# More channel pairs by the usual products while the input's forms are made, in the ffn of a fp32 decoder trunk

## The chip, the core and the metric

The kernel runs on one core of one Trainium2 chip. The metric is the device time of one execution in microseconds (us), lower is better: 1331.78 us is the median of three runs of the kernel before (1330.34 to 1333.43).

## What is computed

A decoder trunk of two layers, on 512 rows of a prompt and 8 x 8 rows of samples (576 columns T in the kernel, which keeps the activations transposed, channels on partitions). Each layer is a mixer and a gated ConvFFN; the change is in the ConvFFN, which is the larger part of both layers:

```python
D_MODEL = 1024
D_FF = 3 * D_MODEL
FFN_CONV = 3

def _conv_ffn(xn, prev, w_up, cw, cb, w_down):
    u = jnp.einsum("btd,df->btf", xn, w_up)
    uc, new_prev = _causal_dwconv(u, prev, cw, cb)
    g, val = jnp.split(uc, 2, axis=-1)
    return jnp.einsum("btf,fd->btd", jax.nn.gelu(g) * val, w_down), new_prev
```

Here xn is the RMS-normed input, w_up is 1024 x 6144, w_down 3072 x 1024. Layer 0 has an attention and RG-LRU mixer (mixer_ab), layer 1 a pooling mixer (mixer_pool). All is float32.

## The kernel before

run() calls mixer_ab, pool_setup (GpSimd makes the band matrices of the pooling mixer), ffn(0), mixer_pool, ffn(1). A fp32 product is made as three products of a high and a low part (hi x hi, hi x lo, lo x hi), each of 128 x 128 weights with 288 columns, two halves for the 576. A weight block is loaded to `wraw`, then split: ScalarE copies the high part, VectorE subtracts it for the low one (split, or wform in the units; both write `whl`).

**ffn, up projection.** The 6144 channels are 24 pairs of blocks of 128: index i, s = 0 the gate, s = 1 the value. For each pair, u is the product, conv (L1256) makes a causal convolution of width 3 of it (ScalarE, then two VectorE operations, L1268 and L1269, on tile t), gate (L1272) applies GELU, multiplies, and leaves the product as a pair hh, hl in `hs[i]`.

- The pairs i = 0 and 1 go by up_pair (L1283): the usual products of mm3, 8 blocks of the input x 3 x 2 halves = 48 matmuls for each s, from the input's parts xs that are there already; the norm's factor rb is multiplied in when u is read out of `pu`.
- The other 22 pairs go by 22 units. A unit n covers the blocks i and i + 1 of one s and forms a 2 x 2 product by seven products instead of eight (named 1 to 7, in the order 1, 2, 5, 6, 7, 4, 3; 12 matmuls each, in the banks X, Y, Z). For that it needs sums and differences of the weights' four quarters (a11 to a22, made on GpSimd, L1390 to L1399) and of the input's quarters.
- The input's forms are made by normed() (L1320), called after up_pair(0), and sums() (L1337), called after up_pair(1). For four chunks c, normed makes xn[c] and xn[c + 4] (VectorE, L1323, 128 x 576), copies their high parts to xa and xb (ScalarE, L1325) and the low parts (VectorE, L1326), then makes four mixed sums in place (GpSimd, L1329 to L1332, 128 x 288). sums() splits what is then in xn to xh and xl.

**ffn, down projection.** The 3072 rows are six blocks q of 512, by eight blocks m of output channels: dn_w loads (`wd`) and splits, dn_p (L1488) makes 4 k x 3 x 2 = 24 matmuls (L1495) and add_x adds the result into xT (VectorE, L711).

**What sets the order.** A list `plan` (L1521 to L1551) holds the products of the units and the down blocks in the order of TensorE. Weights are prepared three entries ahead. Blocks q < 5, 40 in all, stand in it: one after product 6 of each unit from n = 3, one after its product 5 from n = 2, and the rest behind the last unit. After it comes the last block, q = 5 (L1573 on), three m at a time, k = 0, 1 of all three first. tick() runs one step of a background list (`bg`): loads and transposes of convolution states (states), and the transposes and stores of the convolution's tails (tails). A scheduler then fixes the order of each engine's queue from the program and its priorities.

**Space.** xn shares its buffers with hh and hl (tags "hh", "hl", 6 each). xa and xb lie in ffn's own pool.

Of the kernel before, what the change touches and what calls it, by code (L numbers as in the profile page):

```python
# [43 lines left out]
class Trunk:  # L44
# [1179 lines left out]
    def ffn(self, l, after, first=0):  # L1224
# [7 lines left out]
        b8 = lambda t: t.rearrange("p (b j) -> p b j", j=8)  # L1232
        with self.tc.tile_pool(name="ff", bufs=2, reuse_waits="tile") as fp:
            stT = fp.tile([P, 48, 16], F32, name="fstT", bufs=1)
# [8 lines left out]
            for a in (1, 7, 2, 8, 3, 9, 4, 10, 5, 11):  # L1243
                self.bg.append(lambda a=a: states(a))
            if l == 0:
                for a in range(2):
                    self.bg.append(lambda a=a: self.pool_states(fp, a))
# [24 lines left out]
            def gate(i, tg, tv):  # L1272
                A.activation(tg[:, 0:592], tg[:, 0:592], AF.Gelu_apprx_tanh)
                hf_ = self.sm.tile([P, T], F32, name="hf", tag="sq", bufs=2)
                V.tensor_tensor(hf_[:, 0:NP], tg[:, 0:NP], tv[:, 0:NP], MUL)  # L1275
                V.tensor_tensor(b8(hf_[:, NP:T]), b10(tg, 0, 8), b10(tv, 0, 8), MUL)
                hh = fp.tile([P, T], F32R, name="hh", tag="hh", bufs=6)
                hl = fp.tile([P, T], F32R, name="hl", tag="hl", bufs=6)
                A.copy(hh, hf_)
                V.tensor_tensor(hl, hf_, hh.bitcast(F32), SUB)  # L1280
                hs[i] = (hh, hl)

            def up_pair(i):  # L1283

                if i % 2 == 0:
                    for s in range(2):
                        if self.up0:
# [26 lines left out]
            xa, xb = [], []  # L1314
            for p in range(2):
                xa.append(fp.tile([P, 4, HT], F32R, name="xa", tag=f"xa{p}", bufs=1))
                xb.append(fp.tile([P, 4, T], F32R, name="xb", tag=f"xb{p}", bufs=1))
            X = {}

            def normed():  # L1320
                for c in range(4):
                    for k in (c, c + 4):
                        V.scalar_tensor_tensor(xn[k], self.xT[:, k, :], self.g_ffn(l, k), self.rb, MUL, MUL)  # L1323
                    for x, v in ((xa, xn[c][:, 0:HT]), (xb, xn[c + 4])):
# [45 lines left out]
            def load(n, f, h):  # L1370

                if n > 21:
# [3 lines left out]
                c0 = n % 2 * DFF + (2 + n // 2 * 2 + f) * P  # L1376
                nc.sync.dma_start(quarter(n, f, h), up[:, 4 * h:4 * h + 4, c0:c0 + P])
# [5 lines left out]
            def unit(n):  # L1383

                s, i = n % 2, 2 + n // 2 * 2
                a11, a12, a21, a22 = [quarter(n, f, h) for f in range(2) for h in range(2)]
# [77 lines left out]
                def p3(w):  # L1464
# [36 lines left out]
            def tails(q, s):  # L1501
# [17 lines left out]
            sums()  # L1519

            units = {}  # L1521
            downs = deque((q, m) for q in range(5) for m in range(8))
            plan = []
# [10 lines left out]
            put(0, "5")  # L1534
            for n in range(22):
                nx = n + 1 if n < 21 else None
# [28 lines left out]
            for j, (kind, a, b) in enumerate(plan):  # L1565
# [3 lines left out]
                else:  # L1569
                    dn_p(a, b, ready.pop(j))  # L1570
                if kind == "down" or a < 3:
                    self.tick()

            after(None)
            ms = [range(0, 3), range(3, 6), range(6, 8)]
            ws = {}
            for m in range(3):
                ws[m] = dn_w(5, m)
            self.psum(8)
            for g in ms:  # L1580
                ps = {}
                for m in g:
                    ps[m] = dn_p(5, m, ws[m], None, range(2))
                for m in g:
                    dn_p(5, m, ws[m], ps[m], range(2, 4))
                    if m + 3 < 8:
                        ws[m + 3] = dn_w(5, m + 3)
                    after(m)
                    if len(self.bg) > 1:
                        self.tick()  # L1590
                    if self.mid:
                        self.mid.popleft()()
            self.flush()
# [27 lines left out]
    def run(self):  # L1621
        self.load_x()
        self.mixer_ab()
        with self.tc.tile_pool(name="pb", bufs=1, reuse_waits="tile") as pb:
            self.pool_setup(pb)
            self.ffn(0, self.then_norm(lambda m: self.g_mix(1, m)), first=4)
            self.xg_end()
            self.mixer_pool(pb)
        self.xg_end()
# [212 lines left out]
```

## Time and profile before

| | us |
|---|---|
| median of three runs | 1331.78 |
| lowest and highest | 1330.34, 1333.43 |
| the profiled execution | 1323.17 |
| its span in the trace | 1321.5 |

The profiled execution is 8.6 us under the median of the runs. In the trace an ffn can be cut into four windows: the products of the first two pairs (305.6 to 337.4 us in ffn(0), 823.7 to 856.1 in ffn(1)), the first units until their pace is steady (to 422.6, to 943.7), the rest of the units with the down blocks (to 752.2, to 1273.2), the last block (to 788.0, to 1314.9). Between the two ffn is mixer_pool, ahead of them mixer_ab.

How to read a row: PE is TensorE's matmuls, PEld its weight loads, DVE VectorE, ACT ScalarE, POOL GpSimd, SP the engine that issues most loads. "A <- B" behind an idle time says that the engine waited for B. PEclk is the clock that TensorE was granted, 1.00 being 2.4 GHz. Busy matmuls are pipelined, so their durations overlap; the pace is better read from counts over a window.

### The profile page before, as it was taken

To read this page: it belongs to the slowest core of one execution; us is meant where nothing else is said; L and a number is where in the kernel's file an instruction comes from. 1 tells how busy PE (TensorE), PEld (TensorE's weight loads), DVE (VectorE), ACT (ScalarE), POOL (GpSimd) and SP (SyncE) were. 2 spreads that over 40 slices of the span, in tenths; PEclk is the share of its full clock that TensorE was granted. 3 is DMA by queue.
4 is the path that set the end of the run, shared out by engine and by line. 5 is a ranking of instruction groups with operands and counts; after the bars stand their busy time and mean duration, and the time that the engine had idled before them with its cause. 6 is when DMAs were issued, how large, how long until landed. Compare 5 with 4: busy or idle time off the path is not lost.

```text
span 1321.5 us, 23545 instructions
## 1 busy us (share of the span) xinstructions
PE 1242.3 (94%) x8894; PEld 1175.5 (89%) x8894; DVE 1050.5 (79%) x1939; ACT 691.3 (52%) x1365; POOL 500.9 (38%) x738
## 2 busy tenths in 40 slices
PE   7999989999788999999999999967999999999988
PEld 6988878898578999999999989857999999999987
DVE  5857879887977888888888868886798888888862
ACT  5657467764444554555455446344455555455532
POOL 2240064381843444444443002474343444344300
PEclk9999999999688999999999999968999999999999
DMA  5323343332122333223322202302233233323122
GB/s 156 101 67 100 98 148 89 90 107 85 43 58 66 95 92 93 85 89 90 97 89 75 82 17 70 117 22 73 60 94 98 81 94 93 94 77 98 58 65 74
DMA packets 153478, 111.69 MB, mean 85 GB/s; under 512 B 9217, under 2 KB 144521, under 8 KB 153356
## 3 DMA queue, kind: packets, MB, share of 16 engines
q1 hardware_dynamic: 149220, 101.69, 25.6%
q0 software_dynamic: 3072, 8.46, 2.3%
q8 instruction: 70, 1.15, 0.4%
q14 instruction: 44, 0.36, 0.1%
q10 hardware_dynamic: 1072, 0.04, 0.0%
HBM read 104.14 MB, written 6.25 MB: 84 GB/s over the span
## 4 chain that ended last, share of the span: by engine, by line
PE 70%; DVE 16%; ACT 4%; POOL 3%; issue 3%; DMA 2%; SPq 0%; ACTq 0%; DVEq 0%; POOLq 0%
PE mmb L1495 19%; PE pX L1365 18%; PE pY L1365 9%; PE mmb L143 6%; PE mmb L588 5%; PE pZ L1365 4%; DVE whl L1359 4%; DVE t L1268 2%; PE pu L143 2%; DVE hl L1280 1%; PE mmb L911 1%; DVE t L1269 1%; ACT whl L1358 1%; DVE hf L1275 1%; DMA wraw<-in_ffn_w_up 1%
## 5 line engine op out<-in xcount | busy, mean ns | idle before, releaser
L1495 PE MATMUL mmb<-hh,whl 128*128 128x288 f32 x1536 | 285.8, 298 | 13.2 <-DVE xT L711 7.5
L1495 PEld LDWEIGHTS mmb<-hh,whl 128*128 128x128 f32 x1536 | 232.6, 190 | 14.6 <-DVE xT L711 8.0
L1365 PE MATMUL pX<-xh,whl 128*128 128x288 f32 x1056 | 240.3, 303 | 3.7 <-ACT c L1450 2.7
L1359 DVE TENSOR_TENSOR whl<-wraw,whl 128x512 fp32r<-128x512 f32 x264 | 210.8, 819 | 20.4 <-ACT whl L1358 17.5
L1358 ACT CAST whl<-wraw 128x512 fp32r<-128x512 f32 x264 | 156.9, 619 | 93.3 <-PE mmb L1495 51.6
L1365 PEld LDWEIGHTS pX<-xh,whl 128*128 128x128 f32 x1056 | 182.1, 194 | 5.6 <-ACT c L1450 3.6
L1495 PE MATMUL mmb<-hl,whl 128*128 128x288 f32 x768 | 166.5, 298 | 6.5 <-DVE hl L1280 6.5
L1365 PE MATMUL pX<-xl,whl 128*128 128x288 f32 x528 | 159.4, 302 | 5.3 <-DVE xl L1343 5.3
L711 DVE TENSOR_TENSOR xT<-mmb,xT 128x288 f32<-128x288 f32 x208 | 87.0, 449 | 69.9 <-PE mmb L1495 68.1
L1263 POOL COPY ut<-u 128x18 f32<-128x18 f32 x96 | 36.5, 380 | 259.2 <-DVE u L1427 257.5
L1495 PEld LDWEIGHTS mmb<-hl,whl 128*128 128x128 f32 x768 | 124.2, 190 | 8.6 <-DVE hl L1280 8.4
L1268 DVE SCALAR_TENSOR_TENSOR t<-u,par,t 128x592 f32<-128x592 f32 x96 | 99.9, 1042 | 24.6 <-ACT t L1267 24.2
L1365 PE MATMUL pX<-xa,whl 128*128 128x288 f32 x528 | 90.4, 318 | 18.9 <-ACT xa L1325 10.2
L1365 PEld LDWEIGHTS pX<-xl,whl 128*128 128x128 f32 x528 | 102.2, 194 | 6.5 <-DVE xl L1343 6.5
L1267 ACT ACTIVATE t<-u,par 128x592 f32<-128x592 f32 x96 | 84.4, 882 | 36.9 <-DVE u L1427 34.0
L1365 PEld LDWEIGHTS pX<-xa,whl 128*128 128x128 f32 x528 | 80.4, 205 | 22.6 <-ACT xa L1325 11.9
L1269 DVE SCALAR_TENSOR_TENSOR t<-u,par,t 128x592 f32<-128x592 f32 x96 | 96.0, 1000 | 1.5
L1390 POOL TENSOR_TENSOR wraw<-wraw 128x512 f32<-128x512 f32 x44 | 65.3, 1484 | 74.4 <-DMA wraw<-in_ffn_w_up 74.4
L1365 PE MATMUL pZ<-xb,whl 128*128 128x288 f32 x528 | 86.4, 309 | 1.6 <-ACT whl L1358 1.3
L1399 POOL TENSOR_TENSOR wraw<-wraw,d 128x512 f32<-128x512 f32 x44 | 67.8, 1542 | 42.7 <-DVE whl L1359 42.6
L1365 PEld LDWEIGHTS pZ<-xb,whl 128*128 128x128 f32 x528 | 77.1, 197 | 3.9 <-ACT whl L1358 1.7
L1365 PE MATMUL pY<-xb,whl 128*128 128x288 f32 x528 | 78.7, 298 | 0.0
(440 smaller groups left out, 2821.8 us busy)
## 6 DMA issues: line engine op xcount, KB each, us to landing
wraw<-in_ffn_w_up SPq DMA_DIRECT2D x176, 256.0 KB
wd<-in_ffn_w_down SPq DMA_DIRECT2D x48, 512.0 KB
wraw<-in_ab_w_in SPq DMA_DIRECT2D x9, 1024.0 KB
wraw<-in_ab_w_out SPq DMA_DIRECT2D x4, 1024.0 KB
wraw<-in_ffn_w_up SPq DMA_DIRECT2D x4, 1024.0 KB
xt<-in_x_prompt SPq DMA_DIRECT2D x4, 512.0 KB
out_y_p<-y SPq DMA_DIRECT2D x8, 256.0 KB
wraw<-in_ab_w_in SPq DMA_DIRECT2D x2, 512.0 KB
```

Source lines behind the costliest of these rows:

```text
L143: nc.tensor.matmul(ps[hf][:, 0:HT], w[:, k, :], x[:, hf * HT:(hf + 1) * HT], start=(n == 0 and j == 0), stop=(n == K - 1 and j == 2))
L588: PE.matmul(ps[i], x[:, i * P:(i + 1) * P], w[:, k2, :], start=(k == 0 and j == 0), stop=(k == 7 and j == 2))
L711: self.nc.vector.tensor_tensor(x, ps[hf][:, 0:HT], x, ADD)
L1267: A.activation(t, u[:, 2:594], AF.Identity, scale=self.fw(l, 2, ch), bias=self.fb(l, ch))
L1268: V.scalar_tensor_tensor(t, u[:, 1:593], self.fw(l, 1, ch), t, MUL, ADD)
L1269: V.scalar_tensor_tensor(t, u[:, 0:592], self.fw(l, 0, ch), t, MUL, ADD)
L1358: A.copy(f[:, 0], v)
L1359: V.tensor_tensor(f[:, 1], v, f[:, 0].bitcast(F32), SUB)
L1365: PE.matmul(ps[:, 0:HT], w[:, a, k, :], x[b][:, k, :], start=(start and k == 0 and j == 0), stop=(k == 3 and j == 2), skip_group_check=True)
L1390: G.tensor_tensor(a21, a11, a21, SUB)
L1399: G.tensor_tensor(a12, a12, st["d"], SUB)
L1495: PE.matmul(ps[hf][:, 0:HT], w[:, a, k, :], hs[4 * q + k][b][:, hf * HT:(hf + 1) * HT], start=(k == 0 and j == 0), stop=(k == 3 and j == 2))
```

## The change

Six pairs instead of two go by up_pair. The twelve steps of normed (norm, parts, mixed, for each of four chunks) become entries of a list `todo`; two of them are taken after each s of the pairs 1 to 3, and the mixed sums are on VectorE instead of GpSimd. sums() runs inside pair 5. In the pairs 4 and 5, one down block of q = 0 is made after each s (down_now). 18 units are left, with 28 down blocks in the plan: two for the units 1 to 10, 12 and 14, one for 0, 11, 13 and 15, none for 16 and 17. The last 1024 rows (hs 16 to 23) form one last block: eight k for each m, its weights loaded 1 MB for two m; m = 0 and 1 first make k = 0 to 5 of both, then k = 6 and 7, the others go by mm3. hh and hl get nine buffers; xa and xb lie in a side pool that is closed after the units. pool_setup and pool_states move from ahead of ffn(0) to its end. Two empty background steps stand before the transposes of each tail.

```diff
-            xn = [fp.tile([P, T], F32, name="xn", tag=("hh", "hl")[c // 4], bufs=6) for c in range(8)]
+            xn = [fp.tile([P, T], F32, name="xn", tag=("hh", "hl")[c // 4], bufs=9) for c in range(8)]
...
+                    if i:
+                        for _ in range(2):
+                            if todo:
+                                todo.popleft()()
+                    if i >= 4:
+                        down_now()
+                if i == 5:
+                    while todo:
+                        todo.popleft()()
+                    sums()
...
+                def mixed(c):
                     a0, a1 = xn[c][:, 0:HT], xn[c][:, HT:T]
                     b0, b1 = xn[c + 4][:, 0:HT], xn[c + 4][:, HT:T]
-                    G.tensor_tensor(a0, a1, a0, SUB)
-                    G.tensor_tensor(a1, b1, a1, SUB)
-                    G.tensor_tensor(b1, b1, a0, SUB)
-                    G.tensor_tensor(b0, b0, b1, SUB)
...
+                    V.tensor_tensor(a0, a1, a0, SUB)
+                    V.tensor_tensor(a1, b1, a1, SUB)
+                    V.tensor_tensor(b1, b1, a0, SUB)
+                    V.tensor_tensor(b0, b0, b1, SUB)
+
+                for c in range(4):
+                    for f in (norm, parts, mixed):
+                        todo.append(lambda f=f, c=c: f(c))
...
+                                self.bg.extend([lambda: None] * 2)
...
+            def down_now():
+                q, m = downs.popleft()
+                dn_p(q, m, dn_w(q, m))
+                self.tick()
+
             self.psum(3)
-            for i in range(2):
+            fq = side.enter_context(self.tc.tile_pool(name="fq", bufs=1, reuse_waits="tile"))
+            for i in range(6):
                 up_pair(i)
                 if i == 0:
-                    normed()
-            self.up0 = None
+                    normed(fq)
+                if i == 3:
+                    for s in range(2):
+                        self.bg.append(lambda s=s: tails(0, s))
...
-                if n >= 3:
+                if 1 <= n <= 10 or n in (12, 14):
                     put_down()
...
-                if n >= 2:
+                if n < 16:
                     put_down()
...
+            side.close()
+            if l == 0:
+                pb = self.pb = self.pbx.enter_context(self.tc.tile_pool(name="pb", bufs=1, side="right", reuse_waits="tile"))
+                self.pool_setup(pb)
...
+            hx = lambda k: hs[16 + k]
...
+            def dn8(m):
+                if m % 2 == 0:
+                    now["r"] = self.raw(dn[:, 16:24, m * P:(m + 2) * P], 8, 256)
+                return self.split(now["r"][:, :, m % 2 * P:m % 2 * P + P], 8, P)
...
+            for ks in (range(6), range(6, 8)):
+                for m in range(2):
+                    for k in ks:
+                        for j, (a, b) in enumerate(((0, 0), (0, 1), (1, 0))):
+                            for hf in range(2):
+                                PE.matmul(p2[m][hf][:, 0:HT], w2[m][a][:, k, :], hx(k)[b][:, hf * HT:(hf + 1) * HT],
+                                          start=(k == 0 and j == 0), stop=(k == 7 and j == 2))
+                    if k == 7:
+                        ended(m, p2[m])
...
+            for m in range(2, 8):
+                ended(m, self.mm3(*dn8(m), hx, 8))
```

**How the order of the queues moves.** VectorE in ffn(0), behind the first pair's convolution. Before, normed()'s operations stand in one run, with only weight splits (L1359) of the first units between:

```order
L1323 SCALAR_TENSOR_TENSOR xn<-xT,par,rb 128x576
L1280 TENSOR_TENSOR hl<-hf,hh 128x576
L1323 SCALAR_TENSOR_TENSOR xn<-xT,par,rb 128x576
L1326 TENSOR_TENSOR xa<-xn,xa 128x288
L1323 SCALAR_TENSOR_TENSOR xn<-xT,par,rb 128x576
L1326 TENSOR_TENSOR xb<-xn,xb 128x576
L1323 SCALAR_TENSOR_TENSOR xn<-xT,par,rb 128x576
L1359 TENSOR_TENSOR whl<-wraw,whl 128x512 x2
L1326 TENSOR_TENSOR xa<-xn,xa 128x288
L1326 TENSOR_TENSOR xb<-xn,xb 128x576
L1323 SCALAR_TENSOR_TENSOR xn<-xT,par,rb 128x576 x3
L1326 TENSOR_TENSOR xa<-xn,xa 128x288
```

After (xn is L1335 there, the low parts L1340, the mixed sums L1345 to L1348, a pair's u L1312 to L1314, its convolution L1265 and L1266, a pair's weight split L131):

```order
L1340 TENSOR_TENSOR xb<-xn,xb 128x576
L1345 TENSOR_TENSOR xn<-xn 128x288
L1335 SCALAR_TENSOR_TENSOR xn<-xT,par,rb 128x576
L1346 TENSOR_TENSOR xn<-xn 128x288
L1312 TENSOR_TENSOR u<-pu,rb 128x288
L1347 TENSOR_TENSOR xn<-xn 128x288
L1313 TENSOR_TENSOR u<-pu,rb 128x224
L1348 TENSOR_TENSOR xn<-xn 128x288
L1314 TENSOR_TENSOR u<-pu,rb 128x8x8
L1312 TENSOR_TENSOR u<-pu,rb 128x288
L1313 TENSOR_TENSOR u<-pu,rb 128x224
L1314 TENSOR_TENSOR u<-pu,rb 128x8x8
```

The steps now stand among the pairs' own operations, and the mixed sums, which VectorE's queue did not have, between them.

TensorE in ffn(0), at the first unit. Before, the first unit's products stand directly behind the second pair's (L1240 is the transpose of a state):

```order
L143 MATMUL pu<-xl,whl 128x288 x2
L143 MATMUL pu<-xh,whl 128x288 x4
L143 MATMUL pu<-xl,whl 128x288 x2
L143 MATMUL pu<-xh,whl 128x288 x2
L1240 MATMUL mmb<-ident,fst 128x64
L1365 MATMUL pX<-xa,whl 128x288 x4
L1240 MATMUL mmb<-ident,fst 128x64
L1365 MATMUL pZ<-xb,whl 128x288 x3
```

After (the sixth pair's last products, a down block at L1514, then the first unit at L1382):

```order
L143 MATMUL pu<-xl,whl 128x288 x2
L143 MATMUL pu<-xh,whl 128x288 x2
L1514 MATMUL mmb<-hh,whl 128x288 x2
L1514 MATMUL mmb<-hl,whl 128x288 x2
L1514 MATMUL mmb<-hh,whl 128x288 x4
L1514 MATMUL mmb<-hl,whl 128x288 x2
L1514 MATMUL mmb<-hh,whl 128x288 x4
L1514 MATMUL mmb<-hl,whl 128x288 x2
L1514 MATMUL mmb<-hh,whl 128x288 x4
L1514 MATMUL mmb<-hl,whl 128x288 x2
L1514 MATMUL mmb<-hh,whl 128x288 x2
L1382 MATMUL pX<-xa,whl 128x288 x12
L1382 MATMUL pZ<-xb,whl 128x288 x12
```

The first unit now has the pairs 2 to 5 and four down blocks ahead of it, and its products of xa stand twelve in a row.

SP's queue in ffn(0), from the last loads of the pairs to the first quarters of the units' weights. Before (L120 loads a pair's weights, L1485 a down block's, L1238 states, L1377 quarters):

```order
L120 DMA wraw<-in_ffn_w_up 128x8x256
L1099 DMA pst<-in_state_pool 120x512
L1485 DMA wd<-in_ffn_w_down 128x4x256 x2
L120 DMA wraw<-in_ffn_w_up 128x8x256
L1238 DMA fst<-in_state_ffn_conv 64x1x128 x2
L1377 DMA wraw<-in_ffn_w_up 128x4x128 x4
L1238 DMA fst<-in_state_ffn_conv 64x1x128
L1377 DMA wraw<-in_ffn_w_up 128x4x128 x5
L1238 DMA fst<-in_state_ffn_conv 64x1x128 x3
```

After (quarters at L1394, down weights at L1504, the stores of tails at L1526 and L1527):

```order
L1238 DMA fst<-in_state_ffn_conv 64x1x128 x6
L120 DMA wraw<-in_ffn_w_up 128x8x256 x2
L1504 DMA wd<-in_ffn_w_down 128x4x256
L1238 DMA fst<-in_state_ffn_conv 64x1x128
L1394 DMA wraw<-in_ffn_w_up 128x4x128 x3
L1526 DMA out_ffn_conv_p<-tl 2x4x128
L1527 DMA out_ffn_conv_s<-tl 16x4x128
L1394 DMA wraw<-in_ffn_w_up 128x4x128
L1504 DMA wd<-in_ffn_w_down 128x4x256
L1526 DMA out_ffn_conv_p<-tl 2x4x128
```

The quarters now stand behind the loads for the pairs and down blocks, and the stores of the first tails, which need a transpose on TensorE, stand among them.

## Rows read from the trace of the kernel before

**Rows 1.** The page, part 1: busy time, share of the span, instructions of each engine.

```profile
PE 1242.3 (94%) x8894; PEld 1175.5 (89%) x8894; DVE 1050.5 (79%) x1939; ACT 691.3 (52%) x1365; POOL 500.9 (38%) x738
```

**Rows 2.** Windows: length, busy us (instructions) of PE, PEld, DVE, ACT, POOL, PEclk, DMA share, GB/s.

```profile
305.60:337.40 31.80, 30.14 (x216) 27.98 (x214) 24.66 (x45) 15.35 (x25) 10.41 (x17) 1.00 0.27 79
337.40:422.60 85.20, 64.86 (x353) 58.06 (x354) 67.57 (x96) 39.75 (x81) 47.41 (x52) 0.76 0.18 53
337.40:380.40 43.00, 29.37 (x111) 23.38 (x111) 36.84 (x46) 18.53 (x40) 26.98 (x26) 0.60 0.14 42
422.60:752.20 329.60, 326.44 (x2459) 325.38 (x2458) 278.90 (x465) 171.46 (x324) 131.74 (x178) 1.00 0.30 88
752.20:788.00 35.80, 30.90 (x220) 30.39 (x218) 24.32 (x46) 14.56 (x25) 0.22 (x1) 0.95 0.08 24
823.70:856.10 32.40, 31.96 (x216) 29.71 (x216) 26.23 (x45) 13.14 (x24) 15.19 (x20) 0.95 0.43 122
856.10:943.70 87.60, 65.90 (x346) 58.65 (x346) 65.78 (x95) 39.58 (x80) 46.31 (x54) 0.75 0.17 49
943.70:1273.20 329.50, 326.11 (x2459) 325.03 (x2458) 279.68 (x465) 171.24 (x324) 130.19 (x178) 1.00 0.29 86
1273.20:1314.90 41.70, 35.77 (x254) 33.90 (x252) 16.13 (x34) 10.64 (x24) 0.22 (x1) 0.96 0.20 57
```

**Rows 3.** Groups of TensorE, 337.4 to 422.6 us: busy, mean ns | idle before, releasers.

```profile
L1365 PE MATMUL pX<-xh,whl 128*128 128x288 f32 x80 | 21.1, 339 | 2.2 <-ACT c L1450 1.7 <-ACT c L1456 0.5
L1365 PE MATMUL pX<-xa,whl 128*128 128x288 f32 x60 | 15.8, 404 | 8.3 <-ACT xa L1325 4.1 <-DVE xa L1326 3.2 <-DVE whl L1359 0.9
L1365 PE MATMUL pX<-xl,whl 128*128 128x288 f32 x40 | 13.6, 341 | 3.1 <-DVE xl L1343 3.1
```

**Rows 4.** VectorE timeline, from 337 us: start, duration, line, operation.

```profile
337.47 1.82 DVE L1323 SCALAR_TENSOR_TENSOR xn<-xT,par,rb 128x576 f32<-128x576 f32 x1
339.21 0.45 DVE L1326 TENSOR_TENSOR xa<-xn,xa 128x288 fp32r<-128x288 f32 x1
339.58 0.81 DVE L1323 SCALAR_TENSOR_TENSOR xn<-xT,par,rb 128x576 f32<-128x576 f32 x1
...
346.69 0.74 DVE L1326 TENSOR_TENSOR xb<-xn,xb 128x576 fp32r<-128x576 f32 x1
```

**Rows 5.** Windows, instructions on xn alone; columns as in Rows 2.

```profile
305.60:422.60 117.00, 0.00 (x0) 0.00 (x0) 24.73 (x24) 9.40 (x16) 17.93 (x16) 0.82 0.21 60
```

**Rows 6.** Groups of VectorE, 305.6 to 337.4 us: the split of a pair's weights.

```profile
L131 DVE TENSOR_TENSOR whl<-wraw,whl 128x1024 fp32r<-128x1024 f32 x3 | 3.6, 1217 | 0.0
```

**Rows 7.** Windows, tile pu alone: PE, PEld, DVE, then clock and DMA.

```profile
305.60:422.60 117.00, 27.29 (x192) 25.66 (x192) 3.77 (x12) 0.82 0.21 60
```

**Rows 8.** Windows, tile t alone (convolution and gate): DVE, ACT, clock, DMA.

```profile
422.60:752.20 329.60, 90.57 (x112) 46.60 (x57) 1.00 0.30 88
```

**Rows 9.** Groups of VectorE, 422.6 to 752.2 us: hl.

```profile
L1280 DVE TENSOR_TENSOR hl<-hf,hh 128x576 fp32r<-128x576 f32 x18 | 21.4, 1189 | 0.0
```

**Rows 10.** The same view: the sum into xT, the split of a down block.

```profile
L711 DVE TENSOR_TENSOR xT<-mmb,xT 128x288 f32<-128x288 f32 x76 | 31.8, 448 | 15.9 <-PE mmb L1495 15.9
L1359 DVE TENSOR_TENSOR whl<-wd,whl 128x512 fp32r<-128x512 f32 x41 | 27.9, 684 | 3.7 <-ACT whl L1358 3.7
```

**Rows 11.** Waits of TensorE, 422.6 to 752.2 us: total, times, longest.

```profile
PE mmb L1495 <- DVE hl L1280: 3.2, 4, 0.8
```

**Rows 12.** Timeline of VectorE and TensorE in the last block of ffn(0).

```profile
760.56 1.42 DVE L1280 TENSOR_TENSOR hl<-hf,hh 128x576 fp32r<-128x576 f32 x2
...
762.40 0.70 PE L1495 MATMUL mmb<-hh,whl 128*128 128x288 f32 x2 [3.75 <-DVE xT L711]
...
763.37 1.16 PE L1495 MATMUL mmb<-hh,whl 128*128 128x288 f32 x4
...
766.16 0.69 PE L1495 MATMUL mmb<-hh,whl 128*128 128x288 f32 x4
```

**Rows 13.** Windows, the stretch of pool_setup; columns as in Rows 2.

```profile
264.80:297.30 32.50, 31.98 (x262) 30.50 (x259) 28.05 (x62) 19.66 (x46) 28.63 (x100) 1.00 0.31 103
```

More of the change, by code (lines that the diff above doesn't have):

```diff
@@ L1232, in ffn @@
         b8 = lambda t: t.rearrange("p (b j) -> p b j", j=8)
-        with self.tc.tile_pool(name="ff", bufs=2, reuse_waits="tile") as fp:
+        with self.tc.tile_pool(name="ff", bufs=2, reuse_waits="tile") as fp, ExitStack() as side:
             stT = fp.tile([P, 48, 16], F32, name="fstT", bufs=1)
@@ L1244, in ffn @@
                 self.bg.append(lambda a=a: states(a))
-            if l == 0:
-                for a in range(2):
-                    self.bg.append(lambda a=a: self.pool_states(fp, a))
             hs = {}
@@ L1286, in up_pair @@
                     for s in range(2):
-                        if self.up0:
+                        if i == 0 and self.up0:
                             raws[s] = self.up0[0][s]
@@ L1314, in ffn, with normed, norm, parts @@
             xa, xb = [], []
-            for p in range(2):
-                xa.append(fp.tile([P, 4, HT], F32R, name="xa", tag=f"xa{p}", bufs=1))
-                xb.append(fp.tile([P, 4, T], F32R, name="xb", tag=f"xb{p}", bufs=1))
             X = {}
-            def normed():
-                for c in range(4):
+            todo = deque()
+            def normed(fq):
+                for p in range(2):
+                    xa.append(fq.tile([P, 4, HT], F32R, name="xa", tag=f"xa{p}", bufs=1))
+                    xb.append(fq.tile([P, 4, T], F32R, name="xb", tag=f"xb{p}", bufs=1))
+                for t, n in ((xa, "a0"), (xb, "b0")):
+                    X[n] = [v[:, :, 0:HT] for v in t]
+                X["b1"] = [v[:, :, HT:T] for v in xb]
+                def norm(c):
                     for k in (c, c + 4):
                         V.scalar_tensor_tensor(xn[k], self.xT[:, k, :], self.g_ffn(l, k), self.rb, MUL, MUL)
+                def parts(c):
                     for x, v in ((xa, xn[c][:, 0:HT]), (xb, xn[c + 4])):
@@ L1370, in load @@
             def load(n, f, h):
-                if n > 21:
+                if n > 17:
                     return
@@ L1508, in tails @@
                 nc.sync.dma_start(os_[:, cs].rearrange("b (j p) -> b j p", p=P), tl[8:72])
+            downs = deque((q, m) for q in range(4) for m in range(8))
+            def down_now():
+                q, m = downs.popleft()
+                dn_p(q, m, dn_w(q, m))
+                self.tick()
             self.psum(3)
-            for i in range(2):
+            fq = side.enter_context(self.tc.tile_pool(name="fq", bufs=1, reuse_waits="tile"))
+            for i in range(6):
                 up_pair(i)
                 if i == 0:
-                    normed()
-            self.up0 = None
+                    normed(fq)
+                if i == 3:
+                    for s in range(2):
+                        self.bg.append(lambda s=s: tails(0, s))
             for n in range(2):
@@ L1518, in ffn @@
                     load(n, f, h)
-            sums()
             units = {}
-            downs = deque((q, m) for q in range(5) for m in range(8))
             plan = []
@@ L1534, in ffn @@
             put(0, "5")
-            for n in range(22):
-                nx = n + 1 if n < 21 else None
+            for n in range(18):
+                nx = n + 1 if n < 17 else None
                 put(n, "6")
@@ L1544, in ffn @@
                     put(nx, "25")
-                if n >= 2:
+                if n < 16:
                     put_down()
                 put(n, "43")
-            while downs:
-                put_down()
+            assert not downs
             ready = {}
@@ L1570, in ffn @@
                     dn_p(a, b, ready.pop(j))
-                if kind == "down" or a < 3:
+                if kind == "down" or a > 10 and b == "3":
                     self.tick()
-            after(None)
[L1575 to L1578, printed above, removed]
-            self.psum(8)
[L1580 to L1592, printed above, removed]
+            side.close()
@@ new lines, in ffn @@
+            if l == 0:
+                pb = self.pb = self.pbx.enter_context(self.tc.tile_pool(name="pb", bufs=1, side="right", reuse_waits="tile"))
+                self.pool_setup(pb)
+                for a in range(2):
+                    self.bg.append(lambda a=a: self.pool_states(pb, a))
+            after(None)
+            hx = lambda k: hs[16 + k]
+            now = {}
+            def dn8(m):
+                if m % 2 == 0:
+                    now["r"] = self.raw(dn[:, 16:24, m * P:(m + 2) * P], 8, 256)
+                return self.split(now["r"][:, :, m % 2 * P:m % 2 * P + P], 8, P)
@@ new lines, in ended @@
+            def ended(m, ps):
+                self.add_x(m, ps)
+                after(m)
+            w2 = [dn8(m) for m in range(2)]
+            p2 = [(self.bank(), self.bank()) if m else (self.px.tile([P, 512], F32, name="pd", tag="X", bufs=2),
+                                                        self.bank()) for m in range(2)]
+            for ks in (range(6), range(6, 8)):
[7 more added lines that the diff above has]
+                        ended(m, p2[m])
@@ L1623, in run @@
         self.mixer_ab()
-        with self.tc.tile_pool(name="pb", bufs=1, reuse_waits="tile") as pb:
-            self.pool_setup(pb)
+        with ExitStack() as self.pbx:
             self.ffn(0, self.then_norm(lambda m: self.g_mix(1, m)), first=4)
             self.xg_end()
-            self.mixer_pool(pb)
+            self.mixer_pool(self.pb)
         self.xg_end()
```

13 lines of the change are left out of this document (6 added, 7 removed).

## The prediction

> **What bounds the kernel now.** I read the page first. TensorE's matmuls are busy 94% of the span, VectorE 79%, ScalarE 52%, GpSimd 38% [rows 1]: TensorE is the one to watch, and VectorE is not free. A share of the whole span hides stages, so I cut the two ffn parts into windows [rows 2]. The reader is to see three kinds of stage. The long one (422.6 to 752.2, 943.7 to 1273.2) holds 2459 matmuls in 326.4 us of busy time out of 329.6: one per 0.1327 us, at a granted clock of 1.00, the 2.4 GHz level. It goes at TensorE's pace, with VectorE busy 278.9/329.6 = 85%.
>
> The stage ahead of it, 85.2 and 87.6 us, is different. By the code an ffn has 3192 matmuls of this size (two pairs of 96, 22 units of 84, 48 down blocks of 24). 216 of them fall after 752.2, some 2450 in the long stage and 192 ahead of 337.4, so about 336 are left for this one: 44.6 us at 0.1327. So 40.6 us are lost here, and 43.0 in ffn(1). In its first half the clock is 0.60, near the 1.2 GHz level, TensorE is idle 43.0 - 29.4 = 13.6 us, and VectorE is busy 36.8 [rows 2]. The idle groups say what for: most of it for xa and xl [rows 3], forms of the input that normed() and sums() make. VectorE's timeline shows how they are made [rows 4]: the same 576-wide xn takes 1.82 us in one place and 0.81 in another. GpSimd's 16 mixed sums take 17.9 us meanwhile, and VectorE's 24 operations on the same tiles 24.7 [rows 5].
>
> The third place is the last block: 35.8 us for 216 matmuls, which at full pace are 28.7.
>
> **The change, part by part.** The sum is made against the profiled execution, 1323.2 us, which is 8.6 under the median of the runs shown, 1331.8; I carry that difference along unchanged.
>
> *Matmuls.* A pair i (gate and value block) is 96 matmuls; two units (84 each) do two pairs. So four pairs more by the usual products cost 384 instead of 336: 48 more per ffn, 96 in all, 12.7 us at 0.1327. That is a real loss. What it buys is 384 matmuls, and 96 of four down blocks, that need none of the forms and run while these are made.
>
> *Six-pair stage.* The first two pairs keep their 31.8 and 32.4 us. Then come 480 matmuls, 63.7 us. Is VectorE fast enough? A pair has two splits of 1.22 us [rows 6]; u, 3.77 us for four blocks, so 1.9 for two [rows 7]; convolution and gate, 90.6 us for 112 operations, six to a pair, so 4.9 [rows 8]; hl 1.2 [rows 9]. That is 10.4 and, for four pairs, 41.4. Four down blocks: 4 x (0.68 + 2 x 0.45) = 6.3 [rows 10]. The forms: eight xn at 0.81, four xa at 0.45, four xb at 0.74 [rows 4], eight xl at 0.81 like an xn of that size: 17.7. The 16 mixed sums have no row on VectorE. The nearest is the subtraction for xa, of the same 128x288: 0.45, in all 7.2; the upper bound is GpSimd's own 17.9 [rows 5]. I take 7.2, the same engine and width. Sum: 72.6 us of VectorE for 63.7 of TensorE.
>
> The xn rows need weighing here. 1.82 is 1.0 above 0.81, about one GpSimd sum (17.9/16 = 1.1), and the 24 operations took 24.7 where the undisturbed prices give 17.7: 7 us of VectorE's time went into waiting for GpSimd. I take it that this goes when GpSimd has no sums to make, so that 17.7 + 7.2 = 24.9 stands for 24.7 and the sums cost VectorE nothing net. If it stays, VectorE has 79.6. The Trainium skill has the mechanism and a harder price (SBUF — State Buffer, "Who interferes with whom"): a VectorE instruction with two SBUF inputs and a GpSimd one that reads SBUF exclude each other, each for its whole length. By that alone the sums could hold VectorE up for all their 17.9 us, and if that were kept it would have 90.5; the trace bears the rule out in kind, at 7 us.
>
> 72.6 is 8.9 above TensorE's 63.7. But part of it starts beside the second pair, where VectorE is busy only 24.7 of 31.8 us [rows 2], and the last pair's convolution runs on into the units. I put the stall at 7 us; bounds 0 (all hidden) and 30 (79.6 at the long stage's share of 85% is 93.6, less 63.7).
>
> *Units.* 18 units and 28 down blocks are 2184 matmuls, 289.8 us. In the long stage now, 41 down blocks (by their 41 splits of wd) cost VectorE 1.58 each [rows 10], and (2459 - 41 x 24)/84 = 17.6 units the rest: (278.9 - 64.8)/17.6 = 12.2 each. Afterwards it is 18 x 12.2 + 28 x 1.58 = 264, 91% of 289.8. A unit with one down block is 14.3 us of TensorE and 13.8 of VectorE: still TensorE's. The last two units have none, 11.1 against 12.2: 2.2 us lost. The waits for hl, 3.2 us now [rows 11], will not shrink. The first unit's weights are loaded at the hand-over, behind other transfers of SP's queue (its order above), and formed on GpSimd and VectorE: 2 to 3 us. Together 8; bounds 0 and 15.
>
> *Last block.* 384 matmuls, 51.0 us. Now the last hl ends at 762.0, 9.8 us after the last product of the units (752.2); TensorE waits 3.75 us ahead of 762.4 and goes on at half pace: four matmuls take 1.16 us where the same four take 0.69 a little later [rows 12]. After the change 62 matmuls of the blocks m = 0 and 1, for k up to 5, stand in that hole: 8.2 us. The 1 MB weight loads have to be there: at the long stage's 88 GB/s one takes 12 us, with all its DMA share (0.30) taken up 3.6 [rows 2]. I take 6 us of stall; bounds 0 (hole filled, clock kept) and 15 (a load 12 us late, and 3 of waiting). In ffn(1) the output transposes add 41.7 - 35.8 = 5.9, as now.
>
> *Other edits.* pool_setup keeps GpSimd busy 28.6 of 32.5 us ahead of ffn(0), beside matmuls that are busy 32.0 [rows 13]: taking it away there gains nothing. At the end of ffn(0), where GpSimd is idle (busy 0.2 us of 35.8, [rows 2]), 51 us of matmuls cover it. If that cover is gone the pool mixer starts up to 32.5 us late; I cost it at nothing. The two empty background steps only delay the transposes of tails, the larger hs buffers remove waits that the rows do not show.
>
> *Sum.* ffn(0): 31.8 + 63.7 + 289.8 + 51.0 + (7 + 8 + 6) = 457.3 against 31.8 + 85.2 + 329.6 + 35.8 = 482.4, so 25.1 less. ffn(1): 32.4 + 63.7 + 289.8 + 51.0 + 5.9 + 21 = 463.8 against 32.4 + 87.6 + 329.5 + 41.7 = 491.2, so 27.4 less. Together 52.5: 1270.7 for the profiled execution, **1279** for the median.
>
> **The rivals.**
>
> *VectorE becomes the bound of the six pairs.* Its queue, taken in order, now mixes steps of normed() with the splits and convolutions of the pairs. For it: 72.6 against 63.7, and in the long stage it is never fuller than 85%. Against: the prices of the convolution come from a stage in which GpSimd works too, and would fall. If it can be filled to 85% and no more, the stage takes 72.6/0.85 = 85.4 instead of 70.7, 14.7 more per ffn: 1279 + 29 = 1308. With the contention kept as well (93.6) it is 1325.
>
> *Slower: the loss belongs to the start of the units, not to the forms.* The first units need weights through SP's queue, four sums on GpSimd, splits on two engines, on a TensorE at half clock. If that is what costs 40.6 and 43.0 us, it comes back in full after the sixth pair, and the 96 matmuls are added: 1331.8 + 12.7 = 1344.5. It turns the sign when the hand-over loses 26 us per ffn more than the 2 to 3 I give it. For it: whl and c are among the releasers, 0.9 and 2.2 us [rows 3]. Against: xa and xl have 10.4. The Trainium skill would point this way too (Perfetto Trace Analysis, "Identifying the Most-Contended Engine"): judge TensorE by the busy share of its weight loads and work on the fullest engine. By that, weight loads at 89% of the span [rows 1] leave little to win, and a change that adds matmuls should lose their 12.7 us. The windows differ: in the 85.2 us stage the share is 58.1/85.2 = 68%.
>
> *No change.* The stalls of the three places together reach 47 us per ffn instead of 21. Nothing in the rows asks for that much.
>
> **How the numbers follow.** Forecast 0.70, VectorE bound 0.20, slower 0.07, no change 0.03. The forecast's own range: half of the 42 us of stalls gone, 1258, or half as much again, 1300. The 8-in-10 range takes in the VectorE case: 1256 to 1313. A measurement can tell about 0.2% (2.7 us) from no change. Faster 0.90, same 0.03, slower 0.07.
>
> **What would show it.** Right: from the first up product to the first unit product 95 to 105 us, at a clock near 1.00; xn at 0.81 us, mixed sums at 0.45; no waits of TensorE for xa; 290 to 300 us for the units; little idle time of TensorE ahead of k = 6 in the last block. Wrong: more than 10 us of waits for u or whl in the six pairs (VectorE); waits and a low clock at the first unit (the second rival); a pool mixer that waits for GpSimd; a weight load that lands after the last unit.

## The result and the profile after

The changed kernel takes **1276.83 us** (median of four runs, 1269.83 to 1277.54) against 1331.06 (1330.30 to 1333.43): a ratio of 0.9578, 95% interval 0.9542 to 0.9614. Measured once more (label e13_after_again, below) it was 0.9591 [0.9573, 0.9610]. The forecast was 1279, range 1256 to 1313.

The page of the changed kernel, part 1, which answers to [rows 1]:

```profile
PE 1229.1 (96%) x8990; PEld 1170.4 (92%) x8990; DVE 1001.1 (78%) x1891; ACT 665.3 (52%) x1277; POOL 432.9 (34%) x674
```

TensorE has 96 instructions more and is busy 13 us less: its mean granted clock is 0.989 of 2.4 GHz over the span, where it was 0.963. Windows of the changed kernel, columns as in [rows 2]. The cuts are the first up product, the first and the last unit product and the last down product of each ffn:

```profile
310.70:409.90 99.20, 96.97 (x705) 93.21 (x704) 84.32 (x154) 47.88 (x79) 21.34 (x42) 1.00 0.26 79
409.90:716.10 306.20, 296.60 (x2204) 294.62 (x2204) 255.43 (x424) 159.77 (x302) 133.73 (x193) 0.99 0.29 85
716.10:767.90 51.80, 51.24 (x385) 50.50 (x385) 34.04 (x49) 20.94 (x30) 32.00 (x77) 1.00 0.20 63
802.40:909.00 106.60, 102.15 (x705) 97.49 (x705) 86.62 (x155) 46.76 (x79) 24.35 (x47) 0.95 0.29 87
909.00:1213.60 304.60, 295.11 (x2205) 293.12 (x2204) 255.49 (x424) 159.91 (x302) 131.19 (x171) 0.99 0.28 85
1213.60:1269.90 56.30, 54.47 (x412) 53.30 (x411) 20.69 (x34) 15.55 (x27) 0.21 (x1) 1.00 0.24 71
```

| | before | forecast | after |
|---|---|---|---|
| ffn(0): six pairs, units, last block | 482.4 in all | 102.5 + 297.8 + 57.0 = 457.3 | 99.2 + 306.2 + 51.8 = 457.2 |
| ffn(1): the same | 491.2 in all | 103.1 + 297.8 + 62.9 = 463.8 | 106.6 + 304.6 + 56.3 = 467.5 |

The sums of an ffn agree within 4 us; the terms do not. The profiled execution is 46.2 us shorter in span, the two ffn together 48.9. Outside them it is 2.7 us longer: one wait of 4.8 us ahead of ffn(0), in mixer_ab, which the change does not touch, less 1.2 us each in the pool mixer and behind the last product. With that wait ffn(0) begins at 310.7 us, where the traces of the experiments have 300.7 to 307.4 and that of before 305.6. The waits of TensorE from 70 to 95 us in the changed kernel (engine, tile, line <- releaser: total, times, longest):

```profile
PE mmb L1774 <- ACT a__257 L1777: 4.8, 1, 4.8
```

The five longest in the same view, from the first up product to the last unit product of ffn(0):

```profile
PE pX L1382 <- ACT c L1467: 3.4, 1, 3.4
PE mmb L1514 <- DVE hl L1277: 2.7, 3, 0.9
PE mmb L1514 <- DVE xT L711: 2.1, 1, 2.1
PE pu L143 <- DVE whl L131: 1.3, 2, 0.7
PE mmb L1522 <- DVE xT L711: 1.1, 1, 1.1
```

Of the waits for the forms xa and xl in [rows 3] none is left: the forms are ready. One line of the changed kernel for xn and one for the mixed sums (count: min/median/max ns, first and last start):

```profile
L1335 DVE SCALAR_TENSOR_TENSOR xn<-xT,par,rb x16: 800/808/814, 333.5 to 863.4; 128x576 f32<-128x576 f32 x16
```

```profile
L1348 DVE TENSOR_TENSOR xn<-xn x8: 442/446/448, 340.3 to 868.3; 128x288 f32<-128x288 f32 x8
```

The second price was taken from another operation of the same width; 0.45 us was right.

### The profile page after: what moved, and what is told of

It is laid out like the page before. It is cut to its first block, busy times and chain, and to the rows that moved or that the text cites. A ratio compares the mean times of both kernels' runs of the same rounds, so it can differ in the third digit from the quotient of the medians.

```text
span 1275.3 us, 23464 instructions
## 1 busy us (share of the span) xinstructions
PE 1229.1 (96%) x8990; PEld 1170.4 (92%) x8990; DVE 1001.1 (78%) x1891; ACT 665.3 (52%) x1277; POOL 432.9 (34%) x674
## 5 line engine op out<-in xcount | busy, mean ns | idle before, releaser
L1382 PE MATMUL pX<-xh,whl 128*128 128x288 f32 x864 | 192.4, 298 | 6.9 <-ACT c L1467 6.9
L1514 PE MATMUL mmb<-hh,whl 128*128 128x288 f32 x1024 | 190.0, 296 | 4.1 <-DVE xT L711 4.1
L1376 DVE TENSOR_TENSOR whl<-wraw,whl 128x512 fp32r<-128x512 f32 x216 | 155.8, 743 | 25.5 <-ACT whl L1375 23.9
L1514 PEld LDWEIGHTS mmb<-hh,whl 128*128 128x128 f32 x1024 | 154.6, 189 | 4.9 <-DVE xT L711 4.6
L1382 PEld LDWEIGHTS pX<-xh,whl 128*128 128x128 f32 x864 | 144.9, 188 | 8.1 <-ACT c L1467 7.4
L143 PE MATMUL pu<-xh,whl 128*128 128x288 f32 x768 | 143.1, 304 | 2.7 <-DVE whl L131 2.0
L711 DVE TENSOR_TENSOR xT<-mmb,xT 128x288 f32<-128x288 f32 x174 | 72.3, 449 | 75.4 <-PE mmb L143 47.2
L1382 PE MATMUL pX<-xl,whl 128*128 128x288 f32 x432 | 127.7, 296 | 0.0
L130 ACT CAST whl<-wraw 128x1024 fp32r<-128x1024 f32 (+1 forms) x68 | 69.5, 1023 | 106.3 <-PE mmb L143 29.8
L143 PEld LDWEIGHTS pu<-xh,whl 128*128 128x128 f32 x768 | 116.7, 193 | 5.1 <-DVE whl L131 2.6
L1514 PE MATMUL mmb<-hl,whl 128*128 128x288 f32 x512 | 111.8, 298 | 5.5 <-DVE hl L1277 5.5
L1265 DVE SCALAR_TENSOR_TENSOR t<-u,par,t 128x592 f32<-128x592 f32 x96 | 96.3, 1007 | 23.7 <-ACT t L1264 23.4
L131 DVE TENSOR_TENSOR whl<-wraw,whl 128x1024 fp32r<-128x1024 f32 (+1 forms) x68 | 83.3, 1227 | 26.8 <-ACT whl L130 21.5
L1264 ACT ACTIVATE t<-u,par 128x592 f32<-128x592 f32 x96 | 84.3, 882 | 36.3 <-DVE u L1444 22.1
L1266 DVE SCALAR_TENSOR_TENSOR t<-u,par,t 128x592 f32<-128x592 f32 x96 | 90.5, 945 | 1.3
L1514 PEld LDWEIGHTS mmb<-hl,whl 128*128 128x128 f32 x512 | 82.7, 189 | 6.9 <-DVE hl L1277 6.9
L143 PE MATMUL pu<-xl,whl 128*128 128x288 f32 x384 | 84.8, 301 | 1.6 <-DVE xl L293 1.6
L1276 ACT CAST hh<-hf 128x576 fp32r<-128x576 f32 x48 | 32.4, 674 | 96.6 <-DVE hf L1273 95.8
L1382 PEld LDWEIGHTS pX<-xl,whl 128*128 128x128 f32 x432 | 81.4, 188 | 0.0
```

Source lines behind the costliest of these rows:

```text
L130: keep(self.nc.scalar.copy(hi, v))
L131: keep(self.nc.vector.tensor_tensor(lo, v, hi.bitcast(F32), SUB))
L143: nc.tensor.matmul(ps[hf][:, 0:HT], w[:, k, :], x[:, hf * HT:(hf + 1) * HT], start=(n == 0 and j == 0), stop=(n == K - 1 and j == 2))
L711: self.nc.vector.tensor_tensor(x, ps[hf][:, 0:HT], x, ADD)
L1264: A.activation(t, u[:, 2:594], AF.Identity, scale=self.fw(l, 2, ch), bias=self.fb(l, ch))
L1265: V.scalar_tensor_tensor(t, u[:, 1:593], self.fw(l, 1, ch), t, MUL, ADD)
```

## The experiments

Ratios are to the kernel before, run beside on the same chip. Chips differ (before took 1321 to 1326 us there, 1331 beside the result above), so run times are compared on one chip alone, and across chips the ratios.

**e3_two_pairs**, only two pairs, the rest of the change kept.

```diff
-            for i in range(6):
+            for i in range(2):
-            for n in range(18):
+            for n in range(22):
...
-                if 1 <= n <= 10 or n in (12, 14):
+                if 3 <= n <= 17:
...
-                if n < 16:
+                if 2 <= n <= 18:
...
```

> The changed kernel with two pairs only, as before the change (22 units, the steps that are left run behind the second pair), but the mixed sums on VectorE and the new last block. Theory A: the forms are uncovered again, 25 us of VectorE behind 32 us of matmuls and half clock, about 30 us per ffn, less 12.7 us of matmuls: about 1322. Rival C (the loss stays at the start of the units in any case): 1277 - 12.7 = 1264. Rival B (the move of the sums is the gain): also near 1264.

Ratio 0.9812 [0.9790, 0.9834]. The changed kernel was not run on that chip; e1 and e4 below, each one edit away from it, had 0.9596 and 0.9562 there. So the four pairs, with the down blocks' places that go with them, are worth 0.022, 29 us, in spite of 96 more matmuls. C and B alone fall; A had the sign and too large a loss. The stage behind the second pair looks as in [rows 2] again:

```profile
338.80:400.00 61.20, 49.53 (x267) 43.70 (x268) 56.24 (x88) 33.16 (x66) 26.15 (x29) 0.78 0.17 48
```

VectorE is full (56.2 of 61.2), the clock 0.78. From the first up to the last unit product this kernel loses 50.5 us per ffn against its matmuls (2808 x 0.1327 = 372.6 of 423.1); before it was 51.7 and 54.4 (2976, 394.9). So steps and sums on VectorE alone win little here; most of what is left of its gain stands at the end of each ffn (5 and 7 us). Nor is all of the 50.5 us a matter of the forms: 25.8 are lost in the window above (61.2 - 267 x 0.1327) and 5.9 beside the two pairs, but 18.9 later. There the first down block waits for its hh, and the 20 us around it hold 108 matmuls, 14.3 us at full pace:

```profile
PE mmb L1514 <- ACT hh L1276: 3.1, 1, 3.1
```

```profile
400.00:420.00 20.00, 16.88 (x108) 16.63 (x107) 15.87 (x26) 7.80 (x15) 8.87 (x11) 0.83 0.24 68
```

The changed kernel, which has no such wait, loses 15 us in its units (below). So some 4 us per ffn, 8 of the 29, belong to the plan of e3 and not to the cover.

**e1_sums_gpsimd**, the mixed sums back on GpSimd.

```diff
-                    V.tensor_tensor(a0, a1, a0, SUB)
+                    G.tensor_tensor(a0, a1, a0, SUB)
...
```

> The changed kernel with the sixteen mixed sums of each ffn back on GpSimd, all else kept. Theory A (the pairs and down blocks cover the making of the forms): the sums take 17.9 us on GpSimd, now beside some 95 us of matmuls, VectorE loses 7.2 us of work and gains about 7 of contention, the forms are still ready before the first unit: 1277, within 4 us. Rival B (the gain is the move of the sums off GpSimd): 7 to 20 us per ffn come back, 1291 to 1317.

Ratio 0.9596 [0.9580, 0.9612], that of the changed kernel. Theory A holds: with the cover, it does not matter which engine makes the sums. The operations on xn alone in this kernel and, below it, in the changed one (there the 16 sums are among VectorE's 40), columns as in [rows 5]:

```profile
303.00:415.00 112.00, 0.00 (x0) 0.00 (x0) 19.05 (x24) 9.14 (x16) 21.97 (x16) 1.00 0.24 75
310.00:415.00 105.00, 0.00 (x0) 0.00 (x0) 24.11 (x40) 9.11 (x16) 0.00 (x0) 1.00 0.26 78
```

VectorE's 24 operations take 19.1 us, where the kernel before needs 24.7 and the changed kernel 24.1 - 16 x 0.45 = 17.0; the sums on GpSimd take 22.0 instead of 17.9. Spread out, the contention costs VectorE some 2 us and GpSimd 4. That either side can be the one held up is what the Trainium skill states (SBUF — State Buffer, "Who interferes with whom": "Issue order, not op shape, decides who blocks."); the trace agrees in kind.

**e11_no_steps**, all twelve steps at once behind the first pair.

```diff
                     normed(fq)
+                    while todo:
+                        todo.popleft()()
```

> The changed kernel with all twelve steps of normed() given out at once behind the first pair, so that some 20 us of them stand in one run in VectorE's queue ahead of the second pair's u. Theory L (the small steps matter: the two banks of each s hold one pair, so the third pair has to wait for the second's u): 8 to 12 us of waits of pu per ffn, ratio 0.970 to 0.976. Rival M (six pairs are cover enough in any order): 0.958, within 0.002.

Ratio 0.9778 [0.9763, 0.9793]: slower than L's interval, and by 0.019 or 24 us slower than the changed kernel beside it (e13). Waits of TensorE in its six pairs of ffn(1), from the same view as above, and the window of the six pairs in ffn(0):

```profile
PE pu L143 <- DVE u L1314: 6.5, 2, 4.7
PE mmb L1240 <- DMA fst<-in_state_ffn_conv: 3.5, 3, 1.5
```

```profile
301.50:413.40 111.90, 101.33 (x705) 96.85 (x704) 85.32 (x154) 47.92 (x79) 17.11 (x42) 0.92 0.23 70
```

111.9 us instead of 99.2, with the same VectorE work (85.3 against 84.3): the matmuls stand idle 8 us longer, and the clock falls to 0.92. Of the waits u has 6.5 us in ffn(1) and 3.9 in ffn(0), under L's 8 to 12; the loads of the states, which their transposes wait for, have 3.5 and 3.6 (in the changed kernel 0.8 and 0.3). So six pairs are not cover enough without the small steps, but the late u of theory L is only part of it.

**e2_four_pairs and e2b_four_pairs_lag**, four pairs and 20 units, no down blocks among the pairs; in the second the first condition reads 1 <= n <= 12, so the down blocks come a little later.

```diff
-                if 1 <= n <= 10 or n in (12, 14):
+                if n < 12:
-                if n < 16:
+                if n < 20:
...
```

> The changed kernel with four pairs by the usual products instead of six (20 units, no down blocks among the pairs, the same 32 in the plan). Theory A: 48 matmuls fewer in both ffn save 6.4 us; VectorE has 70 us of work for 57 of matmuls, 7 of which fit beside the second pair, so 6 us per ffn are uncovered: about 1277 - 6 + 12 = 1283, with waits at the first unit. Rival C (the loss belongs to the start of the units, whatever stands ahead): 6.4 us faster, 1270.

> Four pairs again, with the down blocks of the plan half a unit to a unit later behind the units that make their rows (one beside unit 0, two for units 1 to 12, one from then on). Four pairs with the earlier plan lost 49 us per ffn, of it about 15 at the first units; waits for hh and for the sums into xT stood in the rest. Theory A (forms uncovered at the first unit, 6 to 15 us, the rest being that plan): ratio 0.962 to 0.968. Rival I (fewer than six pairs lose the whole of it again, whatever the plan): 0.985 as before. Rival C (the start of the units costs the same in any case): 0.953.

Ratios 0.9856 [0.9806, 0.9906] and 0.9681 [0.9651, 0.9711]. The first missed both theories. Its four longest waits in the units of ffn(0):

```profile
PE mmb L1514 <- DVE xT L711: 6.2, 3, 2.1
PE mmb L1514 <- ACT hh L1276: 4.7, 3, 2.6
PE pX L1382 <- ACT c L1467: 4.3, 3, 2.0
PE pX L1382 <- ACT xa L1339: 2.9, 1, 2.9
```

The first two, 10.9 us, are down blocks that stand too close behind the units that make their rows; e2b moves them and has neither wait. The three longest in the same view of e2b:

```profile
PE pX L1382 <- DVE u L1312: 6.1, 1, 6.1
PE pX L1382 <- ACT c L1467: 4.5, 3, 2.5
PE pZ L1382 <- ACT xb L1339: 4.1, 1, 4.1
```

e2b ends at the upper edge of A's interval; I and C fall. xb is a form not ready at the first unit, as theory A had it, and u the pairs' work that VectorE has behind it. Against its matmuls (2832, 375.8 us) e2b loses 32.5 us in ffn(0) up to the last unit product, the changed kernel 26.3 (2856, 379.0); the 3.2 us of matmuls saved do not pay that.

**e8_old_last_block**, the last block of before, q = 4 in the plan.

> The changed kernel with the last block of before: block q = 4 goes into the plan (36 down blocks there, so the last two units have some too), then q = 5 alone, three m at a time. In the traces the end of an ffn, counted against its matmuls at 0.1327 us, lost 7.1 and 13.1 us before and 2.3 and 4.5 after. Theory E (the new last block hides the chain to the last hl and the output transposes): 13 us of that come back, less about 4 for the two units that get down blocks: ratio to the kernel before 0.958 + 0.007 = 0.965. Rival F (the last block is worth nothing, the gain is all at the start of the units): 0.955 to 0.958.

Ratio 0.9629 [0.9599, 0.9660], where E put 0.965; the interval touches that of the changed kernel, so the new block is worth some 5 us, not much more than the measurement can tell. Unit and end windows of ffn(0) (columns as in [rows 2]):

```profile
403.00:721.00 318.00, 310.83 (x2339) 309.45 (x2338) 268.45 (x445) 163.71 (x312) 131.28 (x193) 1.00 0.29 86
721.00:758.00 37.00, 33.44 (x251) 32.70 (x249) 29.93 (x52) 17.27 (x29) 29.81 (x77) 1.00 0.20 58
```

**e4_last_plain**, the first two blocks of the last block one after the other.

```diff
-            for ks in (range(6), range(6, 8)):
+            for ks in (range(8),):
```

> The changed kernel with the first two output blocks of the last block made one after the other (all eight k of m = 0, then m = 1). Theory A: 31 matmuls (4 us) instead of 62 stand in the 10 us chain to the last hl, so 4 us of wait per ffn and some matmuls at half clock: 1285 to 1293. Rival D (the scheduler or the earlier queue fills the hole anyway): 1277, within 3 us.

Ratio 0.9562 [0.9542, 0.9581]: rival D. Its timeline in ffn(0) (mmb is the bank of m = 1, pd of m = 0) has the products of m = 1 ahead of those of m = 0 that need the last hh all the same: the scheduler takes what is ready.

```profile
711.45 0.56 PE L1628 MATMUL mmb<-hh,whl 128*128 128x288 f32 x3
...
716.05 0.40 PE L1628 MATMUL pd<-hh,whl 128*128 128x288 f32 x1 [1.00 <-ACT hh L1276]
```

**e9_two_d, e12_two_d_even_downs and e10_four_pairs_lag_two_d**, a second buffer for d (e10 on top of e2b; e12 moves two down blocks to the last units).

```diff
-                    d = st["d"] = self.res.tile([P, T], F32, name="d", tag="sqacc", bufs=1)[:, 0:512].rearrange(...)
+                    d = st["d"] = (fq.tile([P, 512], F32, name="d", tag="d") if s else self.res.tile(...)[:, 0:512]).rearrange(...)
...
```

The timeline of the changed kernel at the first units, on which it rests: GpSimd's operation on the next d begins as VectorE has read the last one (the profile names no releaser for it), and ScalarE's split waits for what follows it.

```profile
412.12 0.68 DVE L1376 TENSOR_TENSOR whl<-d,whl 128x512 fp32r<-128x512 f32 x1
...
412.93 2.96 POOL L1409 TENSOR_TENSOR d<-wraw 128x512 f32<-128x512 f32 x1 [5.95 <-issue]
...
415.96 1.61 POOL L1411 TENSOR_TENSOR wraw<-d,wraw 128x512 f32<-128x512 f32 x1
...
417.60 0.62 ACT L1375 CAST whl<-wraw 128x512 fp32r<-128x512 f32 x1 [3.73 <-POOL wraw L1411]
```

> The changed kernel with a second buffer for the weight sum d (units of s = 1 use it; hl has eight buffers instead of nine to make room). In the trace of after the first units wait 3.4 us for c, behind a split that waits for GpSimd, whose operation on unit 1's d begins as unit 0's d has been read. Theory G (the one d buffer is what the hand-over still loses): 3.4 us and some half clock per ffn are saved, 7 to 9 us in all, ratio 0.951 to 0.953. Rival H (the loads or GpSimd itself are the next limit): 0.956 to 0.959.

> The changed kernel with the second buffer for d, and the second down blocks of the units 12 and 14 moved to the units 16 and 17, so that no unit is left without one. Theory J (a unit without a down block is VectorE's, 12.2 us against 11.1, with one it is TensorE's): 1 to 3 us per ffn less in the unit stage than with the second d alone, which took 3 to 4 per ffn: ratio 0.948 to 0.953. Rival K (the waits move to the last block, since q = 3 is read later and its buffers come free later): the ratio of the second d alone, 0.955.

> The four pairs with the later down blocks and the second buffer for d together. Theory G: 3 to 4 us per ffn under the four pairs with one buffer, a ratio 0.005 lower than theirs. Rival H: the same ratio as theirs.

Ratios 0.9553 [0.9532, 0.9574], 0.9559 [0.9546, 0.9572] and 0.9657 [0.9632, 0.9681]. Beside e12 the changed kernel had 0.9591 [0.9573, 0.9610], 4.5 us more; e9 had none beside it. So the second d gives about 0.3%, 4 us in both ffn together, which is the fastest version here by little. In e9 the 3.4 us wait for c at that place is gone in ffn(0), the units take 302.3 us instead of 306.2 (in ffn(1) 302.4 instead of 304.6), but 2.8 us of it come back as a wait for u. The result lies between G and H. Under the four pairs it is 3.1 us (e10 against e2b), with intervals that overlap. The even down blocks add nothing to it: J falls.

**e7_no_empty_steps**, without the two empty steps, and **e13_after_again**.

> The changed kernel without the two empty background steps ahead of the tails' transposes. Forecast: they cost and bring nothing, ratio 0.958 within 0.002. Rival N (they spare TensorE a wait for the copy of ut, 3.7 us at one place of the kernel before): 1 to 4 us per ffn slower, 0.960 to 0.964.

> The changed kernel itself once more, beside the runs of this call: every theory expects a ratio of 0.954 to 0.961 to the kernel before. It is the reference for the stages of the other three.

Ratio 0.9585 [0.9570, 0.9600], with 0.9591 for the changed kernel beside it: the steps do nothing, as forecast.

## Why the prediction was right, step by step

*The number.* The gain by the medians is 54.2 us (53.5 in e13), where the sum gave 52.5. Two things that were not forecast stand behind the 1276.8 for 1279. The sum was made for the profiled execution, 1270.7, and that took 1277.0: 3.6 us of the miss lie in the two ffn, the rest in the other 2.7 us named above. And the 8.6 us between profile and median, carried along unchanged, is not there after: the profiled execution takes what the median does. The ratio does not hang on this: 0.960 was forecast, 0.958 and 0.959 are measured on two chips.

*Cover of the forms.* Right, and shown: the waits for xa and xl are gone; with two pairs 0.022 comes back (e3, some 8 of the 29 us by its plan), with all steps in one run 0.019 (e11). The stall of 7 us in ffn(0) measured 99.2 - 31.8 - 63.7 = 3.7; in ffn(1) it was 106.6 - 32.4 - 63.7 = 10.5, at a clock of 0.95 (waits for xl of L293 1.6 us, for states 0.8, for ScalarE 1.2). The 106.6 us lie just outside the 95 to 105 that were to show it. VectorE's 72.6 us were too many: it was busy 84.3 of 99.2 us in the whole stage, 13 less than 72.6 and the 24.7 of the first two pairs. Part of it was moved and not saved (four of the eight xl, the last hl and gate stand behind the first unit product), part was overpriced, hl above all (0.83 us where 1.19 was taken):

```profile
L1277 DVE TENSOR_TENSOR hl<-hf,hh 128x576 fp32r<-128x576 f32 x5 | 4.2, 833 | 0.8 <-ACT hh L1276 0.7
```

*Contention.* Right (xn 0.81 at all 16 places; the 24 operations and the sums take 24.1 us where 24.9 was put). That TensorE gains by it was not claimed, and e1 shows that it does not.

*Units.* The wrong term: 8 us of stall forecast, measured 306.2 - 289.8 = 16.4, of it 1.3 for ten products of the last block that the scheduler put in here: 15. The waits above make up 9.3 of it. Behind the two longest the matmuls go on at half pace for a while, which is another 3 us. Eight products behind the first take 1.92 us, 1.06 at full pace; below them windows of 10 us around both waits, and one without a wait:

```profile
423.80 2.12 PE L1382 MATMUL pZ<-xb,whl 128*128 128x288 f32 x8
425.72 0.45 PE L1382 MATMUL pY<-xh,whl 128*128 128x288 f32 x1
```

```profile
417.90:427.90 10.00, 6.55 (x38) 6.32 (x37) 7.42 (x13) 4.53 (x9) 3.36 (x4) 0.83 0.18 53
639.90:649.90 10.00, 7.95 (x48) 7.96 (x49) 6.42 (x12) 3.18 (x6) 4.11 (x4) 0.83 0.11 32
649.90:659.90 10.00, 10.00 (x78) 10.00 (x77) 8.38 (x13) 6.18 (x12) 4.92 (x8) 1.00 0.27 79
```

The first, 40 matmuls short (5 us), is the wait for c, which is gone in e9 with the second buffer of d, and which I had seen only as "2 to 3 us" of loading at the hand-over. The second, 30 short (4 us), is a down block that waits for VectorE to read its bank (xT L711), where VectorE is full (9.99 of the 10 us ahead). The sum had no wait of that kind among the units, and it is not in e8, nor in e12. That the last two units lose 2.2 us for want of a down block was not borne out (e12). The 2 to 3 us that remain are not settled.

*Last block.* Wrong the other way: 6 us of stall forecast, 51.8 - 374 x 0.1327 = 2.2 measured, in ffn(1) 56.3 - 49.6 = 6.7 with the output transposes, where I had 6 and 5.9. (The 4.5 in e8's forecast comes from a window cut at 1267.6 us, ahead of the last twelve products.) The hole was filled to 0.2 us of wait for hl, the weight loads were there. But e8 shows that this gain is mostly a transfer. From the last unit product of an ffn to the next first up product, or to the end, the changed kernel takes 86.4 and 61.8 us, e8 73.1 and 49.5 with 134 matmuls (17.8 us) less: 4.5 and 5.5 gained. But with six more down blocks among its units (144 matmuls, 19.1 us) e8 takes 318.0 - 19.1 = 298.9 us for them, the changed kernel 306.2 - 1.3 = 304.9; in ffn(1) it is 300.2 against 303.3. So about 9 of the 10 us won at the ends are lost again in the units, in ffn(0) by the wait for xT above and the slower clock behind the waits. My errors of +15 us (units) and -12 us (last blocks) over both ffn are for the most part two sides of one shift, and that they nearly cancel is luck: the sum did not say that stalls would move from the last block into the units.

*Other edits.* pool_setup is hidden: GpSimd is busy 32.0 of the 51.8 us, and the pool mixer behind it takes 34.5 us as against 35.7. That moving it cost or won nothing is read from these rows alone: pool_setup at its old place was not tried, nor were the nine buffers or the down blocks among the pairs by themselves.

*Rivals.* VectorE did not become the bound: it is 85% busy in the six pairs of ffn(0), but the work was less than priced, and 85% is no cap (e3's stage has 92%). The slower one is excluded by its place: the first unit follows the last down block without a wait, and the hand-over costs some 5 us per ffn where 26 were needed. Read as in the prediction, the rule of the Trainium skill (Perfetto Trace Analysis, "Identifying the Most-Contended Engine") would have the 96 matmuls cost their 12.7 us. Here weight loads went from 89% to 92% of the span and the time fell by 4%; in the one stage that counted the share had been 68%.

## What to carry to other kernels

A transform that must be made before a cheaper algorithm can start should be covered by work that doesn't need it, even if that work costs more products: 12.7 us of products bought 29 us net here (e3, some 8 of them by its plan of down blocks). The transform's steps must go into the queue in small pieces among the cover's own work; the same steps in one run cost 24 us (e11). A block that follows too close behind its producers costs more than a better algorithm gives (some 23 us between e2 and e2b, where two pairs fewer save 6.4), so look at the plan's distances first when a variant disappoints.

## What was not expected

Nothing in the code says that two pairs and four pairs differ so little as e3 and e2 do (50.5 and 49.1 us lost per ffn); it was the plan of the down blocks, half a unit of lag being worth 0.0175, some 23 us, with an interval of 0.010 on e2's ratio, from two chips. And the scheduler reorders ready products across two blocks (e4), so a written order of that kind is worth checking before it is kept.
